# Three of eight weight pieces of each gate and up chunk as seven products of 256 columns, and norm weights applied ahead of the transposes

## The chip, the core and the metric

One core of one Trainium2 chip runs one launch of a two-layer decoder trunk. The metric is device time of the launch in microseconds (us), the median of several runs. The profile is one execution of the same program.

## What is computed

Two layers, 256 tokens of width 2048, float32. The mixers (attention and gated delta rule) are not touched here; what matters is the chain around them:

```python
def rms_norm(x, w):
    y = xf * lax.rsqrt(jnp.mean(xf * xf, axis=-1, keepdims=True) + NORM_EPS)
    return (y * w.astype(jnp.float32)).astype(x.dtype)

def swiglu(u, w_gate, w_up, w_down):
    return (jax.nn.silu(u @ w_gate) * (u @ w_up)) @ w_down

for layer in range(DEPTH):
    u = rms_norm(h, mix_norm_pre[layer])
    u = even_mixer(u, ...) if layer % 2 == 0 else odd_mixer(u, ...)
    h = h + rms_norm(u, mix_norm_post[layer])
    u = swiglu(rms_norm(h, ffn_norm_pre[layer]), ffn_w_gate[layer], ffn_w_up[layer], ffn_w_down[layer])
    h = h + rms_norm(u, ffn_norm_post[layer])
```

The gate and up matrices are 2048 x 5632, the down matrix 5632 x 2048.

## The kernel before

**Tiles.** The 256 tokens are two token tiles t = 0 and t = 1 of 128. A weight matrix is cut into chunks of 512 columns, and a chunk into pieces of 256 rows: a piece is 128 partitions x 2 x 512 float32, 512 KB, one DMA. A gate or up chunk has 8 pieces, and there are 11 of each per layer. `load_until` (L186) keeps up to WB = 10 pieces loaded ahead: SyncE (SP) loads a piece into one of RAW = 4 buffers `raw`, ScalarE copies it rounded into `wh` (L179), VectorE writes the rest `raw - wh` into `wl` (L180). Activations are split into a high and a low part in the same way.

**Products.** `step` (L198) takes one piece for one token tile: for each of its 2 blocks of 128 rows three matmuls of 512 columns, `xh wh` (L205), `xh wl` (L206) and `xl wh` (L207), all into the chunk's PSUM tile `acc`, of which there are 3. So a piece costs 12 matmuls of 512 columns for both token tiles. Each matmul loads its own weights, the 128 x 128 activation block.

**Order.** Six phases follow each other: mixer input, mixer output, feed-forward part (FFN), and the same for layer 1. `run_phase` (L228) lets t = 0 run 4 to 8 steps ahead of t = 1, so that what ends t = 0 can lie beside matmuls of t = 1. In the FFN, `plan_ffn` (L443) orders gate and up chunks in pairs and puts the four down chunks of the pair before behind the next gate chunk. The program is written in this order, and a scheduler of the language then orders each engine's instructions by priorities; each engine runs its own in that order.

**Between phases.** `post_residual` (L294) waits for the sums of squares of all four column tiles (`rms`, through GpSimd), adds the scaled result to x (L304), transposes x (L174) and splits it. The norm weight goes in there: after the transpose it is one number per partition, so `transposed` (L248) splits 16 pieces of 128 x 128 for a token tile, ScalarE at L182 and VectorE at L183. The factor 1/rms of the next norm (`prenorm_factor`, L261) isn't needed yet: it is applied to the outputs, in `gate_chunk` (L469) and `up_chunk` (L478) by `self.r[t]`. x stays in SBUF through the FFN.

**Chunk ends.** Gate: one SiLU on ScalarE (L469). Up: one multiply on VectorE (L478), four transposes (L174), a split. Down: one add on VectorE (L496).

## Time and profile before

| | us |
|---|---|
| median of 3 runs | 2458.36 (2457.79 to 2459.09) |
| the profiled execution | 2455.95 |
| its span in the trace | 2454.2 |
| TensorE busy in it | 2415.8 |
| VectorE busy in it | 1359.1 |
| ScalarE busy in it | 1137.3 |

The page gives busy time by engine, the span in 40 slices with the clock that TensorE was granted, and the chain of work that ended last. A matmul's row has its start and a modelled duration; the durations of neighbours overlap, so the cost of one is the distance from one start to the next. Windows are counted from the span's start: the first FFN runs from about 530 to 1286, the second from about 1688 to 2445.

### The profile page before, as it was taken

Reading aid. Unit: us, or ns where it says so; the run is one execution under the profiler, and the core shown is the slowest. Engines: PE = TensorE matmul, PEld = TensorE weight load, DVE = VectorE, ACT = ScalarE, POOL = GpSimd, SP = SyncE. Lnnn points to the kernel's source line nnn. Section 1 sums busy time; section 2 is a strip of 40 time slices with the busy share of each in tenths; the row PEclk is TensorE's granted clock in tenths of the full one; section 3 lists DMA queues with packets and bytes.
Section 4 is the critical chain, followed back from the end, with each engine's and each line's share of the span. In section 5 each row is a group of like instructions: output and inputs, shape, how many; then the busy total and the mean of one; then the engine's idle time right before and its main releaser. Section 6 shows DMA issues by size and latency. Waiting matters only on the chain.

```text
span 2454.2 us, 29318 instructions
## 1 busy us (share of the span) xinstructions
PE 2415.8 (98%) x11076; PEld 1969.2 (80%) x11076; DVE 1359.1 (55%) x1767; ACT 1137.3 (46%) x1558; POOL 189.5 (8%) x212
## 2 busy tenths in 40 slices
...
GB/s 238 209 136 149 142 138 151 146 176 197 183 186 189 181 189 187 185 185 188 193 209 194 163 176 172 200 198 144 204 185 184 184 184 194 180 189 185 186 195 129
DMA packets 128078, 441.90 MB, mean 180 GB/s; under 512 B 14848, under 2 KB 20224, under 8 KB 127936
## 3 DMA queue, kind: packets, MB, share of 16 engines
...
HBM read 435.77 MB, written 4.19 MB: 179 GB/s over the span
## 4 chain that ended last, share of the span: by engine, by line
PE 90%; POOL 2%; DVE 2%; issue 2%; DMA 2%; ACT 1%; POOLq 0%; ACTq 0%; DVEq 0%; SPq 0%
PE acc L207 28%; PE acc L205 28%; PE acc L206 28%; PE p L174 2%; POOL m L838 1%; POOL m L840 1%; PE p L932 1%; ACT wh L179 1%; DVE wl L180 0%; DVE m L304 0%; DMA raw<-in_ev_w_in 0%; PE p L660 0%; PE p L687 0%; PE p L941 0%; POOL m L501 0%
## 5 line engine op out<-in xcount | busy, mean ns | idle before, releaser
L180 DVE TENSOR_TENSOR wl<-raw,wh 128x1024 fp32r<-128x1024 f32 (+1 forms) x808 | 990.7, 1229 | 854.9 <-ACT wh L179 852.9
L179 ACT ACTIVATE wh<-raw 128x1024 fp32r<-128x1024 f32 (+1 forms) x808 | 848.6, 1051 | 956.9 <-PE acc L207 924.9
L205 PE MATMUL acc<-wh,m 128*128 128x512 f32 (+1 forms) x3232 | 1276.7, 396 | 10.7 <-ACT m L182 10.4
L207 PE MATMUL acc<-wh,m 128*128 128x512 f32 (+1 forms) x3232 | 1272.6, 396 | 4.1 <-DVE m L183 4.1
L206 PE MATMUL acc<-wl,m 128*128 128x512 f32 (+1 forms) x3232 | 1274.0, 395 | 0.0
L205 PEld LDWEIGHTS acc<-wh,m 128*128 128x128 f32 x3232 | 609.5, 189 | 151.1 <-ACT m L182 14.2
L207 PEld LDWEIGHTS acc<-wh,m 128*128 128x128 f32 x3232 | 609.5, 189 | 147.3 <-DVE m L183 8.5
L206 PEld LDWEIGHTS acc<-wl,m 128*128 128x128 f32 x3232 | 609.5, 189 | 138.1
L277 POOL DMA_DIRECT2D m<-in_ffn_norm_post x16 | 9.0, 562 | 1405.1 <-PE acc L207 1319.6
L496 DVE TENSOR_TENSOR m<-m,acc 128x512 f32<-128x512 f32 x80 | 54.8, 685 | 61.4 <-PE acc L207 61.4
L174 PE MATMUL p<-ident,m 128*128 128x128 f32 x528 | 77.4, 275 | 1.0 <-ACT m L874 0.6
L174 PEld LDWEIGHTS p<-ident,m 128*128 128x128 f32 x528 | 64.5, 142 | 14.3 <-ACT m L874 1.3
L179 ACT ACTIVATE m<-p 128x512 fp32r<-128x512 f32 x44 | 26.3, 598 | 72.9 <-PE p L174 72.7
L180 DVE TENSOR_TENSOR m<-p,m 128x512 fp32r<-128x512 f32 x44 | 30.4, 691 | 44.1 <-ACT m L179 44.1
L469 ACT ACTIVATE m<-acc,pr 128x512 f32<-128x512 f32 x44 | 30.4, 690 | 45.8 <-PE acc L207 45.8
L290 ACT ACTIVATE m<-m 128x512 f32<-128x512 f32 x48 | 30.1, 628 | 43.6 <-DVE m L496 37.4
L182 ACT ACTIVATE m<-p,nw 128x128 fp32r<-128x128 f32 x128 | 38.6, 376 | 14.3 <-PE p L174 8.7
L561 ACT ACTIVATE m<-acc,pr 128x512 f32<-128x512 f32 x36 | 24.8, 689 | 42.6 <-PE acc L207 42.5
L183 DVE SCALAR_TENSOR_TENSOR m<-p,nw,m 128x128 fp32r<-128x128 f32 x128 | 38.0, 343 | 6.7 <-ACT m L182 6.3
L478 DVE SCALAR_TENSOR_TENSOR m<-acc,pr,m 128x512 f32<-128x512 f32 x44 | 32.9, 748 | 9.6 <-PE acc L207 9.6
L846 DVE SCALAR_TENSOR_TENSOR m<-c,conv,m 128x128 f32<-128x128 f32 x96 | 30.6, 378 | 0.0
L932 PE MATMUL p<-m,m 128*128 128x128 f32 x112 | 20.7, 303 | 8.2 <-POOL m L917 7.7
...
## 6 DMA issues: line engine op xcount, KB each, us to landing
raw<-in_ffn_w_gate SPq DMA_DIRECT2D x176, 512.0 KB, 3.3
raw<-in_ffn_w_up SPq DMA_DIRECT2D x176, 512.0 KB, 3.3
raw<-in_ffn_w_down SPq DMA_DIRECT2D x176, 512.0 KB, 3.3
raw<-in_ev_w_in SPq DMA_DIRECT2D x104, 512.0 KB, 3.9
raw<-in_od_w_in SPq DMA_DIRECT2D x96, 512.0 KB, 3.3
raw<-in_ev_w_out SPq DMA_DIRECT2D x32, 512.0 KB, 4.3
raw<-in_od_w_out SPq DMA_DIRECT2D x32, 512.0 KB, 4.3
...
```

The costliest lines, as they stand in the source:

```text
L174: self.nc.tensor.transpose(o[:, j * P:(j + 1) * P], src[:, j, :], self.ident)
L179: self.nc.scalar.activation(h, src, AF.Copy)
L180: self.nc.vector.tensor_sub(l, src, h.bitcast(F32))
L182: self.nc.scalar.activation(h, src, AF.Copy, scale=scale)
L183: self.nc.vector.scalar_tensor_tensor(l, src, scale, h.bitcast(F32), op0=ALU.mult, op1=ALU.subtract)
L205: nc.tensor.matmul(acc, xh, s.wh[:, j], start=(s.first and j == 0), stop=False)
L206: nc.tensor.matmul(acc, xh, s.wl[:, j], start=False, stop=False)
L207: nc.tensor.matmul(acc, xl, s.wh[:, j], start=False, stop=(s.last and j == 1))
L478: nc.vector.scalar_tensor_tensor(u, acc, self.r[t], u, op0=ALU.mult, op1=ALU.mult)
L496: nc.vector.tensor_add(y, y, acc)
L846: nc.vector.scalar_tensor_tensor(dst[:, h], c[:, h, j:j + P], w[:, j:j + 1], dst[:, h] if j else self.zero, op0=ALU.mult, op1=ALU.add)
L932: mm(z[:, i * P:(i + 1) * P], M[:, i], self.blocks(Xt_, i, s, 1), start=True, stop=True)
```

## The change

Let a piece's two row blocks be split into column halves: B11, B12 for the first block, B21, B22 for the second, each 128 x 256, and let e and o be a token tile's two activation blocks. Strassen's algorithm in Winograd's form gets the products of both token tiles with all four from 7 products instead of 8. 3 of the 8 pieces (NSP) of all gate and up chunks but each layer's first gate chunk go this way (`FastChunk`, `fast_step`), 63 pieces per layer. `split_sums` makes the three weight sums in the `raw` tile with 512, 256 and 256 columns on VectorE; the split then goes over 1792 columns rather than 1024, and the piece takes two of the 10 weight places. The other operand's four sums are made once per layer for 3 pieces in `sums_of_tiles` and transposed (12 transposes of 128 x 128 per layer). A fast step is for both token tiles at once: 7 x 3 matmuls of 256 columns, into 4 PSUM tiles. At the end of a chunk the parts are put together by one copy on ScalarE and six adds on VectorE.

For the sums the activations must be normed whole before the transposes. So the norm weights come in as rows broadcast over partitions (`norm_weights`, through a DRAM tile `nwd` that the start fills), and `post_residual` multiplies by them ahead of the transposes; towards the FFN it multiplies by the factor 1/rms too, so that `prenorm_factor` now stands ahead of the transposes. The boundary splits are then 512 columns wide. `post_residual` gets a high priority (LEAD). `raw` tiles are twice as wide and 3 rather than 4; the SBUF tiles are 44 rather than 48; x is stored to DRAM at the end of a mixer output and loaded again late in the FFN. In an FFN phase three PSUM tiles are lent from the pool `ps` to the pool of accumulators, and given back after the phase.

```diff
-NTILES = 48
+NORMS = (("mix_norm_pre", 0), ("mix_norm_pre", 1), ("ffn_norm_pre", 0), ("ffn_norm_pre", 1))
+NTILES = 44
 NPS = 5
 PSA = 3
-RAW = 4
+RAW = 3
+NSP = 3
+LEAD = 500
+PS_FFN = 3
...
+class FastChunk(Chunk):
+    def __init__(self, pieces, lhs, done):
+        super().__init__(pieces[NSP:], lhs, done)
+        for s in self.steps:
+            s.last = False
+        self.steps += [Step(s, k, self, i == 0, i == NSP - 1, i) for i, (s, k) in enumerate(pieces[:NSP])]
...
+    def lend(self, other):
+        i = self.free.pop()
+        make = self.make if isinstance(i, int) else i[0]
+        other.free.append((make, i if isinstance(i, int) else i[1]))
...
-    def load_until(self, n):
-        nc = self.nc
-        while self.loaded < min(n, len(self.steps)):
+    def load_until(self, n, end=None):
+        nc = self.nc
+        while self.loaded < min(n + WB if end is None else end, len(self.steps)):
             s = self.steps[self.loaded]
-            n_ = s.src.shape[2]
-            raw, wh, wl = (p.tile([P, 2, 512], dt, name=tag, tag=tag)[:, :, :n_] for p, dt, tag in (
-                (self.rpool, F32, "raw"), (self.wpool, F32R, "wh"), (self.wpool, F32R, "wl")))
-            nc.sync.dma_start(out=raw, in_=s.src)
-            self.split(wh, wl, raw)
-            s.wh, s.wl = wh, wl
+            if sum(a.places for a in self.steps[n:self.loaded + 1]) > WB:
+                break
+            raw = self.rpool.tile([P, 2048], F32, name="raw", tag="raw")
+            w = [self.wpool.tile([P, 2048], F32R, name="w", tag="w") for i in range(s.places)]
+            if s.pair is None:
+                n_ = s.src.shape[2]
+                raw = raw[:, :1024].rearrange("p (k n) -> p k n", k=2)[:, :, :n_]
+                s.wh, s.wl = (a.rearrange("p (k n) -> p k n", k=2)[:, :, :n_] for a in (w[0][:, :1024], w[0][:, 1024:]))
+                nc.sync.dma_start(out=raw, in_=s.src)
+                self.split(s.wh, s.wl, raw)
+            else:
+                nc.sync.dma_start(out=raw[:, :1024], in_=s.src.rearrange("p k n -> p (k n)"))
+                self.split_sums(raw.rearrange("p (b n) -> p b n", b=8), s, *w)
             self.loaded += 1
+    def split_sums(self, b, s, wh, wl):
+        nc = self.nc
+        nc.vector.tensor_sub(b[:, 4:6], b[:, 0:1].broadcast_to([P, 2, 256]), b[:, 1:3])
+        nc.vector.tensor_sub(b[:, 6], b[:, 1], b[:, 5])
+        nc.vector.tensor_sub(b[:, 7], b[:, 3], b[:, 6])
+        s.wh, s.wl = (a.rearrange("p (b n) -> p b n", b=8)[:, :7] for a in (wh, wl))
+        self.split(s.wh, s.wl, b[:, 1:8])
     def step(self, t, s):
         nc, ch = self.nc, s.chunk
         if s.first:
...
+    def fast_step(self, s):
+        nc, ch = self.nc, s.chunk
+        if s.first:
+            ch.p16, ch.p57 = self.now(self.pa, 2)
+        lo, hi = slice(0, 256), slice(256, 512)
+        ke, ko = s.kts
+        B11, B22, B21, T1, T3, T2, T4 = range(7)
+        S = lambda i: tuple(a.bitcast(F32R)[:, s.pair * P:s.pair * P + P] for a in self.S[i])
+        products = ((ch.p16[:, lo], ch.lhs(0, ke), B11), (ch.p16[:, hi], S(1), T2),
+                    (ch.p57[:, lo], S(0), T1), (ch.p57[:, hi], S(2), T3),
+                    (ch.acc[0][:, hi], ch.lhs(0, ko), B21), (ch.acc[0][:, lo], S(3), B22),
+                    (ch.acc[1][:, hi], ch.lhs(1, ko), T4))
+        for i, (acc, (xh, xl), b) in enumerate(products):
+            kw = dict(skip_group_check=True)
+            nc.tensor.matmul(acc, xh, s.wh[:, b], start=s.first and i in (0, 2), stop=True, **kw)
+            nc.tensor.matmul(acc, xh, s.wl[:, b], start=False, stop=True, **kw)
+            nc.tensor.matmul(acc, xl, s.wh[:, b], start=False, stop=True, **kw)
+        if s.last:
+            za, zb, zu = self.now(self.mem, 3)
+            u = zu[:, lo]
+            nc.scalar.activation(za[:, hi], ch.p16[:, lo], AF.Copy)
+            nc.vector.tensor_add(u, za[:, hi], ch.p16[:, hi])
+            nc.vector.tensor_add(za[:, lo], u, ch.p57[:, lo])
+            nc.vector.tensor_add(zb[:, hi], u, ch.p57[:, hi])
+            nc.vector.tensor_add(zb[:, lo], zb[:, hi], ch.p57[:, lo])
+            self.mem.give(zu)
+            out = [za, zb]
+            for z, acc in zip(out, ch.acc):
+                nc.vector.tensor_add(z, z, acc)
+            self.pa.give(ch.p16, ch.p57, *ch.acc)
+            ch.done(out)
         self.advance()
...
+            if n0 < hi and self.steps[n0].pair is not None:
+                if n0 == n1:
+                    self.fast_step(self.steps[n0])
+                    n0 += 1
+                    n1 += 1
+                    self.load_until(n1)
+                    continue
+                lag = 0
...
+    def transposed(self, src, n=4):
+        o = self.now(self.ps)
+        for j in range(n):
+            self.nc.tensor.transpose(o[:, j * P:(j + 1) * P], src[:, j * P:(j + 1) * P], self.ident)
+        h, l = self.now(self.mem, 2)
+        self.split(h.bitcast(F32R)[:, :n * P], l.bitcast(F32R)[:, :n * P], o[:, :n * P])
+        self.ps.give(o)
+        return h, l
+    def sums_of_tiles(self, xn):
+        nc = self.nc
+        tiles = self.now(self.mem, 4)
+        S = [a[:, :NSP * P].rearrange("p (i d) -> p i d", d=P) for a in tiles]
+        for c in range((NSP + 1) // 2):
+            n = min(2, NSP - 2 * c)
+            (e0, o0), (e1, o1) = ([v4(xn[t][c]).rearrange("p (i k) d -> p i k d", k=2)[:, :n, j] for j in range(2)]
+                                  for t in range(2))
+            s1, s2, s3, s4 = (a[:, 2 * c:2 * c + n] for a in S)
+            nc.vector.tensor_add(s1, e1, o1)
+            nc.vector.tensor_sub(s2, s1, e0)
+            nc.vector.tensor_sub(s3, e1, e0)
+            nc.vector.tensor_sub(s4, o0, s2)
+        self.S = []
...
-    def post_residual(self, t, norm):
+    def norm_weights(self, which, layer):
+        self.nwb = self.now(self.mem, 4)
+        for c in range(4):
+            self.norm_weight(self.nwb[c], which, layer, c)
+    def post_residual(self, t, then):
         nc = self.nc
         self.free_aT(t)
@@ -302,14 +444,31 @@
         for c in range(4):
             x, y = self.x[t][c], self.y[t][c]
             nc.vector.scalar_tensor_tensor(x, y, rf, x, op0=ALU.mult, op1=ALU.add)
-            self.mem.give(y)
-            if norm is None:
+            if then == "out":
                 nc.sync.dma_start(out=self.out[t * P:(t + 1) * P, c * 512:(c + 1) * 512], in_=x)
-            else:
-                self.transposed(t, c, norm)
-        self.y[t] = None
-        if norm is not None:
+            elif then == "in":
+                nc.vector.tensor_mul(y, x, self.nwb[c])
+                self.aT[t].append(self.transposed(y))
+            if then != "ffn":
+                self.mem.give(y)
+        if then != "out":
             self.prenorm_factor(t)
+        if then == "ffn":
+            for c in range(4):
+                y = self.y[t][c]
+                nc.vector.scalar_tensor_tensor(y, self.x[t][c], self.r[t], self.nwb[c], op0=ALU.mult, op1=ALU.mult)
+                self.aT[t].append(self.transposed(y))
+            if t == 1:
+                self.sums_of_tiles(self.y)
+                for b in range(2):
+                    self.mem.give(*self.y[b])
+        if t == 1 and then != "out":
+            self.mem.give(*self.nwb)
...
-        for (lo, hi), end in zip(bounds, ends):
+        for i, ((lo, hi), end) in enumerate(zip(bounds, ends)):
+            if i % 3 == 2:
+                for j in range(PS_FFN):
+                    self.ps.lend(self.pa)
+                if i == 2:
+                    self.mem.give(*self.lev)
             self.run_phase(lo, hi, end)
+            if i % 3 == 2:
+                for j in range(PS_FFN):
+                    self.pa.lend(self.ps)
...
+    def fast(name, f):
+        return f > 0 or name == "ffn_w_up"
...
+        self.nc.scalar.activation(self.sg[t], acc, AF.Silu)
+    def gate_fast(self, out):
+        self.sg = out
+        for a in out:
+            self.nc.scalar.activation(a, a, AF.Silu)
     def up_chunk(self, t, i, acc):
-        nc = self.nc
-        if i == 0:
-            for pair in self.hT[t]:
-                self.mem.give(*pair)
-            self.hT[t] = []
         u = self.sg[t]
-        nc.vector.scalar_tensor_tensor(u, acc, self.r[t], u, op0=ALU.mult, op1=ALU.mult)
-        o = self.now(self.ps)
-        self.transpose4(o, v4(u))
+        self.nc.vector.tensor_mul(u, acc, u)
+        self.hT[t].append(self.transposed(u))
...
+    def up_fast(self, i, f, out):
+        if f == NFC - 1:
+            self.free_S()
+            for t in range(2):
+                self.free_aT(t)
+        for t in range(2):
+            self.up_chunk(t, i, out[t])
+            self.mem.give(out[t])
...
-        self.post_residual(t, None if layer else 1)
+        with self.tc.high_priority(offset=LEAD):
+            self.post_residual(t, "out" if layer else "in")
         if layer == 0:
-            for c in range(4):
-                self.nc.sync.dma_start(out=self.xd[t * P:(t + 1) * P, c * 512:(c + 1) * 512], in_=self.x[t][c])
-            self.mem.give(*self.x[t])
+            self.store_x(t)
...
-        self.post_residual(t, 2 + layer)
+        with self.tc.high_priority(offset=LEAD):
+            self.post_residual(t, "ffn")
+        self.store_x(t)
...
```

**TensorE, from the first FFN into the second layer's mixer.** p_10107 to p_10155 and p_10788 to p_10810 are transposes of t = 0; the rows ahead of them are t = 1's last matmuls of the down chunk, those behind them t = 0's first of the mixer. Before:

```order
L206 MATMUL acc<-wl,m_9871 128x512
L207 MATMUL acc<-wh,m_9872 128x512
L174 MATMUL p_10107<-ident,m_4192 128x128 x4
L174 MATMUL p_10123<-ident,m_4193 128x128 x4
L174 MATMUL p_10139<-ident,m_4194 128x128 x4
L174 MATMUL p_10155<-ident,m_4195 128x128 x4
L205 MATMUL acc<-wh,m_10112 128x512
L206 MATMUL acc<-wl,m_10112 128x512
L207 MATMUL acc<-wh,m_10113 128x512
```

With the change:

```order
L263 MATMUL p_10905<-w,m_10513 128x512
L364 MATMUL p_10788<-ident,m_10570 128x128 x4
L364 MATMUL p_10799<-ident,m_10660 128x128 x4
L261 MATMUL acc_11034<-w,m_10793 128x512
L262 MATMUL acc_11034<-w,m_10793 128x512
L261 MATMUL acc_11103<-w,m_10793 128x512
L262 MATMUL acc_11103<-w,m_10793 128x512
L364 MATMUL p_10810<-ident,m_10742 128x128 x4
L263 MATMUL acc_11034<-w,m_10794 128x512
```

Four transposed tiles stood in a row, each in a PSUM tile of its own; now two stand there, and the third, which takes the first one's PSUM tile, stands behind four matmuls and ahead of the first use of a low half.

**VectorE, from the first mixer output into the first FFN.** This is the end of t = 0: x is made (L304, L446), and the low halves of its transposes (L183 before, L218 with p in it now) are written. acc at L549 and acc_4643 at L752 are t = 1's last chunk. Before:

```order
L304 SCALAR_TENSOR_TENSOR m_4194<-m_4596,prf,m_4194 128x512
L304 SCALAR_TENSOR_TENSOR m_4195<-m_4703,prf,m_4195 128x512
L180 TENSOR_TENSOR wl<-raw,wh 128x1024 x3
L163 TENSOR_SCALAR pj,pv<-xss 128x5
L180 TENSOR_TENSOR wl<-raw,wh 128x1024
L183 SCALAR_TENSOR_TENSOR m_4725<-p_4719,nw,m_4724 128x128
```

With the change:

```order
L446 SCALAR_TENSOR_TENSOR m_4068<-m_4560,prf,m_4068 128x512
L218 TENSOR_TENSOR w<-raw,w 128x1024 x3
L201 TENSOR_SCALAR pj,pv<-xss 128x5
L190 SCALAR_TENSOR_TENSOR pna<-pny,pv 128x1
L194 TENSOR_SCALAR pna<-pna 128x1
L396 TENSOR_TENSOR pr<-pny,pna 128x1
L459 SCALAR_TENSOR_TENSOR m_4081<-m_4065,pr,m_4073 128x512
L459 SCALAR_TENSOR_TENSOR m_4297<-m_4066,pr,m_4074 128x512
L459 SCALAR_TENSOR_TENSOR m_4457<-m_4067,pr,m_4075 128x512
L459 SCALAR_TENSOR_TENSOR m_4560<-m_4068,pr,m_4076 128x512
```

```order
L218 TENSOR_TENSOR w<-raw,w 128x1024 x2
L201 TENSOR_SCALAR pj,pv<-xss 128x5
L752 TENSOR_TENSOR m_4727<-acc_4643,m_4727 128x512
L218 TENSOR_TENSOR m_4606<-p_4600,m_4605 128x512
```

The second fence follows the first without a gap: between x and the first low half there now stand the whole second norm, four multiplies and t = 1's last output tile.

**VectorE, in the middle of the first FFN.** m_6216 is an up chunk's output before; m_10289 and m_10290 are the two token tiles' outputs of a gate chunk now. Before:

```order
L496 TENSOR_TENSOR m_5647<-m_5647,acc 128x512
L180 TENSOR_TENSOR wl<-raw,wh 128x1024 x5
L478 SCALAR_TENSOR_TENSOR m_6216<-acc,pr,m_6216 128x512
L180 TENSOR_TENSOR wl<-raw,wh 128x1024 x2
L180 TENSOR_TENSOR m_6677<-p_6671,m_6676 128x512
```

With the change:

```order
L218 TENSOR_TENSOR w<-raw,w 128x1024 x3
L292 TENSOR_TENSOR m_10291<-m_10289,acc_10210 128x256
L247 TENSOR_TENSOR raw<-raw 128x512
L293 TENSOR_TENSOR m_10289<-m_10291,p_10211 128x256
L294 TENSOR_TENSOR m_10290<-m_10291,p_10211 128x256
L248 TENSOR_TENSOR raw<-raw 128x256
L247 TENSOR_TENSOR raw<-raw 128x512
L299 TENSOR_TENSOR m_10289<-m_10289,p_10119 128x512
L295 TENSOR_TENSOR m_10290<-m_10290,p_10211 128x256
L249 TENSOR_TENSOR raw<-raw 128x256
```

The next chunk's weight sums (L247 to L249) now stand among the adds that wait for the chunk's last matmuls.

## Rows read from the trace of the kernel before

**Rows 1.** The page: TensorE, its weight loads, VectorE, ScalarE and GpSimd over the span.

```profile
PE 2415.8 (98%) x11076; PEld 1969.2 (80%) x11076; DVE 1359.1 (55%) x1767; ACT 1137.3 (46%) x1558; POOL 189.5 (8%) x212
```

**Rows 2.** Window inside the first FFN: each engine's busy time, granted clock, DMA.

```profile
core 0: us, PE busy (x) PEld busy (x) DVE busy (x) ACT busy (x) POOL busy (x), PEclk, DMA share, GB/s
550.00:1280.00 730.00, 730.00 (x3181) 589.29 (x3180) 372.39 (x346) 307.64 (x323) 12.45 (x15) 1.00 0.57 187
```

**Rows 3.** Timeline of TensorE in the first FFN: start, duration, matmuls of 512 columns.

```profile
799.68 0.40 PE L205 MATMUL acc<-wh,m 128*128 128x512 f32 x1
...
805.99 0.39 PE L205 MATMUL acc<-wh,m 128*128 128x512 f32 x1
```

**Rows 4.** Timeline of TensorE in the first mixer: matmuls of 256 columns, two stretches.

```profile
77.48 0.28 PE L205 MATMUL acc<-wh,m 128*128 128x256 f32 x1
...
80.77 0.28 PE L206 MATMUL acc<-wl,m 128*128 128x256 f32 x1
...
81.59 0.28 PE L205 MATMUL acc<-wh,m 128*128 128x256 f32 x1
...
84.31 0.28 PE L205 MATMUL acc<-wh,m 128*128 128x256 f32 x1
```

**Rows 5.** Chain of waits: eight matmuls of 128 columns (start, time on the chain).

```profile
1378.38 0.89 PE p L687 x8
```

**Rows 6.** Groups by line and shape, VectorE and ScalarE: count, busy us, mean ns.

```profile
L180 DVE TENSOR_TENSOR wl<-raw,wh 128x1024 fp32r<-128x1024 f32 x792 | 979.6, 1239 | 853.8 <-ACT wh L179 851.7
L180 DVE TENSOR_TENSOR wl<-raw,wh 128x544 fp32r<-128x544 f32 x8 | 5.8, 720 | 0.3 <-ACT wh L179 0.3
L674 DVE TENSOR_TENSOR m<-m,sd 128x512 f32<-128x512 f32 x12 | 8.3, 692 | 0.4
L934 DVE TENSOR_TENSOR m<-p,m 128x256 f32<-128x256 f32 x28 | 11.8, 420 | 6.2 <-PE p L932 6.0
L179 ACT ACTIVATE wh<-raw 128x1024 fp32r<-128x1024 f32 x792 | 838.3, 1060 | 947.1 <-PE acc L207 915.5 <-DMA raw<-in_ev_w_in 11.3 <-DMA raw<-in_od_w_out 4.0
L179 ACT ACTIVATE wh<-raw 128x544 fp32r<-128x544 f32 x8 | 5.3, 658 | 5.3 <-PE acc L207 4.8 <-DMA raw<-in_ev_w_abz 0.5
```

**Rows 7.** DMA issues: KB each, median us from issue to landing.

```profile
raw<-in_ffn_w_gate SPq DMA_DIRECT2D x176, 512.0 KB, 3.3
raw<-in_od_w_out SPq DMA_DIRECT2D x32, 512.0 KB, 4.3
```

**Rows 8.** Windows at the three phase boundaries around an FFN.

```profile
529.00:541.00 12.00, 9.19 (x39) 6.49 (x38) 11.86 (x34) 9.91 (x27) 2.12 (x4) 0.86 0.78 263
1286.00:1299.00 13.00, 9.97 (x38) 6.75 (x37) 13.00 (x36) 10.60 (x30) 6.99 (x6) 0.74 0.86 307
1687.00:1700.00 13.00, 10.44 (x41) 7.31 (x40) 12.77 (x36) 10.81 (x30) 2.00 (x3) 0.78 0.70 240
```

**Rows 9.** TensorE's timeline at the first: sixth and nineteenth matmul behind the transposes.

```profile
532.40 0.39 PE L207 MATMUL acc<-wh,m 128*128 128x512 f32 x1
...
540.61 0.39 PE L205 MATMUL acc<-wh,m 128*128 128x512 f32 x1
```

**Rows 10.** Timeline of VectorE at the same place: start, time, instructions.

```profile
519.96 0.69 DVE L549 TENSOR_TENSOR m<-acc,m 128x512 f32<-128x512 f32 x1 [4.82 <-ACT m L290]
...
524.28 2.73 DVE L304 SCALAR_TENSOR_TENSOR m<-m,prf,m 128x512 f32<-128x512 f32 x4
526.93 3.49 DVE L180 TENSOR_TENSOR wl<-raw,wh 128x1024 fp32r<-128x1024 f32 x3
...
531.55 0.86 DVE L183 SCALAR_TENSOR_TENSOR m<-p,nw,m 128x128 fp32r<-128x128 f32 x3
```

**Rows 11.** Timeline at the start: SP's weight loads, VectorE's first weight split.

```profile
8.14 1.62 SPq L193 DMA_DIRECT2D raw<-in_ev_w_in  x2
...
9.24 1.22 DVE L180 TENSOR_TENSOR wl<-raw,wh 128x1024 fp32r<-128x1024 f32 x1 [9.24 <-ACT wh L179]
...
13.04 2.62 SPq L193 DMA_DIRECT2D raw<-in_ev_w_in  x2
```

100 lines of the change are left out of this document (70 added, 30 removed).

## The prediction

> **What bounds the kernel now.** I read the page's busy times first: TensorE is busy for 98% of the span, no other engine for more than 55% [rows 1]. Then a window inside the first FFN, where the change acts: TensorE is busy for all of its 730 us, at a granted clock of 1.00, which is the upper of its two levels, 2.4 GHz, while VectorE works 372 us of them, 51%, and the DMA engines 57% [rows 2]. So in the FFN the time is the number of matmuls times the distance between two. That distance comes from the timeline: from 799.68 to 805.99 there are 27 steps, so 0.2337 us for 512 columns [rows 3]; over longer stretches it comes out at 0.233, which I use. Last I looked where TensorE does wait near an FFN: at the three boundaries around it, where its share falls to 77 to 80% and its mean clock to 0.74 to 0.86 [rows 8]. There VectorE is the one that is busy, 98 to 100% of the window.
>
> **The products.** A piece now takes 12 matmuls of 512 columns: 12 x 0.233 = 2.80 us. A fast piece takes 21 of 256 columns. The trace has such matmuls, each with its own weight load and with the same pattern of operands (the same block twice, then its low part): 28 steps from 77.48 to 80.77 make 0.1175 us, 24 steps from 81.59 to 84.31 make 0.1133 [rows 4]. I take 0.1165, half of 0.233 and nearer to the slow stretch: 21 x 0.1165 = 2.45 us. That is 0.35 us less per piece, and for 2 layers x 21 chunks x 3 = 126 pieces 44 us; with the two measured ends it is 42 to 53 us. TensorE was without a gap there, so all of it lies on the path, if the operands are there in time.
>
> **A rule against it.** Matmuls of 128 columns, a quarter of 512, come every 0.111 us (0.89 us for eight) [rows 5], not every 0.058, so something other than columns has a floor there, and 256 columns lie just above it. The Trainium skill, "TensorE: Matmul & The Clock Gate", section "LDWEIGHTS (loading the stationary operand)", gives a load of 128 columns 128/1.2 = 107 ns. By that the load fills nearly the whole of a 256-column matmul, and were it not hidden the gain would turn into a loss (second rival below); if hidden, the sum stays at -44 us. The two stretches of rows 4 speak for hidden.
>
> **What TensorE gets in addition.** 12 transposes of the activation sums per layer and one of the norm weights: 25 x 0.111 [rows 5] = +2.8 us, on its path.
>
> **The boundaries.** The first costs 5.2 us: from 532.40 to 540.61 there are 13 steps, 8.2 us where 3.0 would do [rows 9]. For the others I add TensorE's idle time (3.0 and 2.6 us) and half of the time at the lower level, 1.2 GHz: a mean of 0.74 over 13 us is 6.8 us of it, 0.78 is 5.7 [rows 8]. That makes 6.4 and 5.5, and 17 for all three. What decides is when VectorE writes the first low halves, since L207, now L263, waits for them. t = 0's last output is taken up at 519.96 and x is written from 524.28 on, behind a norm with two weight splits in it; then come three splits (3.49 us) and one more, and the first low quarter at 531.55 [rows 10]. In the new order those two splits are gone from the norm, so x starts 2.3 us earlier, at 522.0. Then follow four x (2.73), three splits (3.49), the second norm with its trip through GpSimd (3.6 us from 520.65 to 524.28 for the first, less its two splits: 1.3), four multiplies (2.7), two splits (2.3), t = 1's output (0.7) and the low half (0.7): 535.9, some 4 us later than before. But it is a whole 512 columns then, and the next three follow 0.7 to 1.8 us apart, where the 16 small pieces kept TensorE waiting again and again. So TensorE waits in one piece of about 4 us, and gets the lower clock behind it as before: I put this at +1.5 us at each of the two mixer-output boundaries. Behind the FFN the third transpose needs the first one's PSUM tile, which is free only after that tile's split; the queue up to there holds six weight splits (7.0 us), eight tiles of x and y (5.4), three adds and two multiplies of outputs (3.4), a norm (1.3) and the split (0.7): some 18 us after t = 0's last matmul, of which t = 1's 39 matmuls cover 9. That is some 7 us idle beside the transposes, and up to 3.4 lost at the lower clock, against 6.4 before: +4. Together +7. The bounds are -9 (the priority clears VectorE's queue and half of the 17 us go) and +16 (twice my delay).
>
> **The start.** The fourth weight load now waits until the first buffer is free, at about 10.5 rather than 8.1, and what stands behind it on SP, two x tiles and the fifth load (13.04 before), moves by as much [rows 11]. TensorE waits for x there: +2 us, between 0 and 4. In the mixers the loads have 3 buffers too, but the order of their small matmuls among the large is within a few steps of before: 0, within 3 either way.
>
> **Weights in time.** This is what a fast chunk hides behind matmuls, and it costs nothing only while VectorE keeps up. A chunk takes TensorE 60 x 0.233 + 63 x 0.1165 = 21.3 us. VectorE: a fast piece needs 0.69 + 0.42 + 0.42 for the sums, and a split of 1792 columns, by 1239 and 720 ns at 1024 and 544 columns about 2.05: 3.6 us; three of them and five ordinary splits (1.24) make 17.0 us; the chunk's end four adds of 256 and two of 512 columns, 3.1; an up chunk two multiplies and two splits more, 2.8 [rows 6]. That is 20 to 23 us in durations, some 8% less in sequence, since three splits in a row take 3.49 us, not 3.72 [rows 10]. So VectorE is full while four fast chunks follow each other, and has its pause in the four down chunks behind them (45 us of matmuls, about 25 of VectorE). What lies ready ahead is ten places, some six pieces or 15 us. A raw tile is held for 3.3 (landing [rows 7]) + 1.5 + 1.7 (ScalarE's 1060 and 658 ns carried on to 1792) + 2.05 = 8.6 us by a fast piece, 5.6 by another [rows 6]: 54 us per chunk over 3 tiles, 18 against 21.3. It fits by a little; I give it +2 us, between 0 and 12. The reloads of x and norm weights go through GpSimd's queue, which has 190 us of work in the whole span [rows 1], a group ahead of their use: 0. The stores of x stand on SP ahead of weight loads, but wait only for x, which is early: 0.
>
> **Sum.** -44 + 2.8 + 7 + 2 + 2 = -30. The profiled execution took 2455.95 us (its span 2454.2 and 1.75 around it), the median is 2.4 above it: 2458.4 - 30 = 2428 us.
>
> **Rivals.** First, the boundaries get cheaper: rows 8 show VectorE at 98 to 100% there, with weight splits among it, and the boundary's own work has become 12 wide operations from 20 small and wide ones per token tile. At -9 instead of +7 the time is 2412 us. Against it: the order still has five splits ahead of the first low half. Second, the load isn't hidden behind 256 columns: then a product takes 0.1165 + 0.111 = 0.228 us, a piece 4.8, and the time is 2428 + 126 x 2.3 = about 2720 us; from 2.80/21 = 0.133 per product on the change does not do what it says and nothing is gained. Rows 4 speak against both. Third, and slower: VectorE and the three raw tiles become the bound in the fast chunks. A piece that waits one and a half times for another's split holds its tile for 3.1 us more, which makes 26 us per chunk; four in a row are late by 19 us, of which the lead hides some 10, eleven such runs give +100: about 2530 us. It is slower than before from some 24.5 us per chunk on. For it: VectorE at 92 to 100% by my sum, and a landing of 4.3 us is seen elsewhere [rows 7]. Against it: splits of the next chunk stand ahead of TensorE's need by some 6 us in the order, and DMA is busy 57% [rows 2]. A mild form of it, 5 to 25 us, gives 2435 to 2453.
>
> **How the numbers follow.** Forecast 0.64; cheaper boundaries 0.17; the mild form of the third rival 0.10, its strong form 0.07; loads not hidden 0.02. The forecast's own bounds, with products at -53 to -42, boundaries from 0 to +16, start, mixers and weights at their ends, reach from 2415 to 2446. The range takes in the first rival and leaves out the strong third, the second and the upper part of the mild one: 2410 to 2447. Faster by over 0.2% (4.9 us, about what a measurement of this kernel can tell from no change) is the forecast, the first rival and nearly all of the mild form: 0.88; within 0.2% 0.04; slower 0.08.
>
> **What would show it.** Steps of 0.113 to 0.118 us at L285 to L287 at a clock of 1.00, and TensorE without gaps in the FFN windows, VectorE there at about 80%: right. A row of TensorE waiting for VectorE at L287 or L285 behind a chunk's third piece: the third rival. At the boundaries one wait of 3 to 5 us for L218, 7 behind the FFN, with a clock of 0.7 to 0.9 behind it: right; none: the first rival. Most likely wrong is the boundaries' sum, since it hangs on when weight splits are ready; what would break the forecast is a fast chunk above 21.3 us.

## The result and the profile after

The changed kernel takes 2477.59 us (median of 4 runs, 2473.97 to 2480.75) against 2458.69 for the kernel before: a ratio of 1.0077, 95% interval 1.0059 to 1.0094. It is 19 us slower; 30 us faster was forecast, and the range ended at 2447. The profiled execution took 2476.57 us (span 2474.8), 20.6 more than that of before.

From the page after, the lines that answer to [rows 1] and [rows 7], and the shares of the chain of work that ended last:

```profile
PE 2393.2 (97%) x12235; PEld 1992.8 (81%) x12235; DVE 1725.7 (70%) x2373; ACT 1205.3 (49%) x1537; POOL 201.3 (8%) x241
PE 28%; DMA 24%; DVE 19%; ACT 6%; issue 4%; ACTq 0%; POOL 0%; DVEq 0%; POOLq 0%
DVE w L218 12%; DMA raw<-in_ffn_w_gate 9%; DMA raw<-in_ffn_w_down 8%; DMA raw<-in_ffn_w_up 7%; ACT w L217 6%; PE acc L263 5%; PE acc L261 5%; PE acc L262 5%; PE p L263 3%; PE p L262 3%; PE p L261 3%; DVE m L299 1%; DVE raw L247 1%; DVE raw L248 1%; DVE raw L249 1%
raw<-in_ffn_w_gate SPq DMA_DIRECT2D x176, 512.0 KB, 4.2
```

The chain's shares by engine before:

```profile
PE 90%; POOL 2%; DVE 2%; issue 2%; DMA 2%; ACT 1%; POOLq 0%; ACTq 0%; DVEq 0%; SPq 0%
```

TensorE is still busy for 97% and no other engine for more than 70%, so the first line hides what happened. The chain shows it: 90% of its time was TensorE's before, now 28% is; weight loads have 24% and weight splits 18% (12 on VectorE, 6 on ScalarE). A load lands after 4.2 us where it took 3.3.

The fast products are there and as cheap as forecast. TensorE's timeline inside a fast chunk, the first and the last of 63 rows (start, modelled duration):

```profile
791.00 0.28 PE L285 MATMUL acc<-w,m 128*128 128x256 f32 x1
...
798.04 0.28 PE L287 MATMUL acc<-w,m 128*128 128x256 f32 x1
```

62 steps in 7.04 us are 0.1135 each; the mean over the run is 0.115. What the page can't show is where TensorE waited. I took, for every matmul of the trace, the step to the next one's start less what it takes undisturbed (0.233 us for 512 columns, 0.115 for 256, 0.123 for 272, 0.111 for 128), and added it up by stretch of the span. A wait and the lower clock behind it are both in it. With three of the kernels that follow:

| lost by TensorE, us | before | b_raw3_nt44 | a_nofast | after | a_raw4 |
|---|---|---|---|---|---|
| start (0 to 60) | 9.4 | 8.0 | 8.6 | 8.6 | 8.6 |
| mixer and its output (60 to 500) | 25.5 | 40.6 | 39.6 | 41.2 | 29.6 |
| first boundary (500 to 560) | 5.0 | 7.3 | 4.5 | 4.4 | 7.1 |
| inside the first FFN (560 to 1230) | -0.2 | 0.0 | -0.5 | 13.9 | -1.6 |
| its last down chunks, FFN to mixer (1230 to 1400) | 6.4 | 18.1 | 7.0 | 22.0 | 8.6 |
| odd mixer, third boundary (1400 to 1740) | 6.1 | 6.3 | 5.8 | 4.4 | 5.8 |
| second FFN (from 1740) | -0.6 | -0.4 | 0.4 | 22.2 | 0.2 |
| sum | 51.6 | 80.0 | 65.4 | 116.7 | 58.2 |

TensorE lost 65 us more than before and had 45 less to do. Its waits in after, by what ended them: us in total, times, longest.

```profile
PE p L364 <- DVE m L450: 7.0, 1, 7.0
PE p L261 <- ACT w L217: 5.7, 1, 5.7
PE acc L261 <- ACT w L217: 5.6, 2, 4.8
PE p L364 <- DVE m L666: 5.5, 4, 2.4
PE acc L364 <- DVE m L666: 4.0, 4, 1.7
```

Two of these are weights that came late in the last down chunks of each FFN (L261 for L217, 4.8 and 5.7 us). The eight of L364 for L666 recur once in each pair of gate and up chunks, some 135 us apart: the product of gate and up is late on VectorE. In a_raw4 below, the first kind has 0.3 us left and the second nothing.

**One late load.** SP, VectorE and ScalarE around the end of that fast chunk; the loads and subtractions are those of the next chunk's fast pieces (timeline; in brackets the idle time ahead and what ended it):

```profile
794.46 4.59 SPq L240 DMA_DIRECT2D raw<-in_ffn_w_gate  x3
807.06 10.94 SPq L237 DMA_DIRECT2D raw<-in_ffn_w_up  x5
...
801.31 0.69 DVE L247 TENSOR_TENSOR raw<-raw 128x512 f32<-128x512 f32 x1 [0.69 <-DMA raw<-in_ffn_w_gate]
801.92 0.41 DVE L293 TENSOR_TENSOR m<-m,p 128x256 f32<-128x256 f32 x1
802.25 0.41 DVE L294 TENSOR_TENSOR m<-m,p 128x256 f32<-128x256 f32 x1
802.58 0.42 DVE L248 TENSOR_TENSOR raw<-raw 128x256 f32<-128x256 f32 x1
803.14 0.69 DVE L247 TENSOR_TENSOR raw<-raw 128x512 f32<-128x512 f32 x1
803.75 0.68 DVE L299 TENSOR_TENSOR m<-m,acc 128x512 f32<-128x512 f32 x1
804.34 0.41 DVE L295 TENSOR_TENSOR m<-m,p 128x256 f32<-128x256 f32 x1
804.67 0.42 DVE L249 TENSOR_TENSOR raw<-raw 128x256 f32<-128x256 f32 x1
805.01 2.02 DVE L218 TENSOR_TENSOR w<-raw,w 128x1792 fp32r<-128x1792 f32 x1
...
805.18 1.70 ACT L217 ACTIVATE w<-raw 128x1792 fp32r<-128x1792 f32 x1 [2.76 <-DVE raw L249]
```

The piece whose first subtraction starts at 801.31 has its third one end at 805.09, 3.8 us later, though the three take 1.53: between them stand the adds of the chunk's end (L293 to L299) and the next piece's first subtraction. The three raw tiles are taken from 798.7 on, and SP issues no load until a split ends at 807.03: the next goes out at 807.06. From 60 us on nearly every load goes out 0.03 us after the split that frees its tile, so a tile's holding time is the distance from its issue to the third issue behind it. Over 560 to 1230 that is 13.24 us for the 63 fast pieces and 6.81 for the 172 others; the prediction had 8.6 and 5.6. A fast chunk's loads then take (3 x 13.24 + 5 x 6.81) / 3 = 24.6 us, TensorE 21.2. The four down chunks behind four fast ones win most of that back: their 16 loads hold a tile for 6.75 us each, 36.0 us over three tiles, for 44.7 us of TensorE. So a group of eight chunks falls 4 x 3.4 - 8.7 = 4.9 us short, and the five groups of an FFN some 25 us, an estimate from these means; against a_nofast the table has 29 us for the first FFN with the stretch behind it and 22 for the second.

### The profile page after: what moved, and what is told of

The parts are those of the page before. It is cut to its first block, busy times and chain, and to the rows that moved or that the text cites. A ratio compares the mean times of both kernels' runs of the same rounds, so it can differ in the third digit from the quotient of the medians.

```text
span 2474.8 us, 32450 instructions
## 1 busy us (share of the span) xinstructions
PE 2393.2 (97%) x12235; PEld 1992.8 (81%) x12235; DVE 1725.7 (70%) x2373; ACT 1205.3 (49%) x1537; POOL 201.3 (8%) x241
## 4 chain that ended last, share of the span: by engine, by line
PE 28%; DMA 24%; DVE 19%; ACT 6%; issue 4%; ACTq 0%; POOL 0%; DVEq 0%; POOLq 0%
DVE w L218 12%; DMA raw<-in_ffn_w_gate 9%; DMA raw<-in_ffn_w_down 8%; DMA raw<-in_ffn_w_up 7%; ACT w L217 6%; PE acc L263 5%; PE acc L261 5%; PE acc L262 5%; PE p L263 3%; PE p L262 3%; PE p L261 3%; DVE m L299 1%; DVE raw L247 1%; DVE raw L248 1%; DVE raw L249 1%
## 5 line engine op out<-in xcount | busy, mean ns | idle before, releaser
L218 DVE TENSOR_TENSOR w<-raw,w 128x1024 fp32r<-128x1024 f32 (+2 forms) x808 | 1085.7, 1350 | 551.8 <-ACT w L217 548.9
L217 ACT ACTIVATE w<-raw 128x1024 fp32r<-128x1024 f32 (+2 forms) x808 | 928.7, 1153 | 993.3 <-DVE raw L249 231.5
L261 PE MATMUL acc<-w,m 128*128 128x512 f32 (+2 forms) x1622 | 643.2, 397 | 14.6 <-ACT w L217 5.6
L262 PE MATMUL acc<-w,m 128*128 128x512 f32 (+2 forms) x1622 | 640.4, 396 | 4.0 <-DVE w L218 3.9
L263 PE MATMUL acc<-w,m 128*128 128x512 f32 (+2 forms) x1622 | 639.9, 396 | 2.0 <-DVE m L218 1.2
L261 PE MATMUL p<-w,m 128*128 128x512 f32 x1106 | 439.8, 399 | 6.8 <-ACT w L217 5.7
L262 PE MATMUL p<-w,m 128*128 128x512 f32 x1106 | 439.3, 397 | 4.0 <-DVE w L218 3.7
L263 PE MATMUL p<-w,m 128*128 128x512 f32 x1106 | 438.5, 397 | 0.2 <-DVE m L218 0.2
L261 PEld LDWEIGHTS acc<-w,m 128*128 128x128 f32 x1622 | 307.6, 190 | 84.2 <-ACT w L217 7.9
L262 PEld LDWEIGHTS acc<-w,m 128*128 128x128 f32 x1622 | 307.5, 190 | 75.2 <-DVE w L218 9.4
L263 PEld LDWEIGHTS acc<-w,m 128*128 128x128 f32 x1622 | 307.5, 190 | 70.6 <-DVE m L218 1.8
L261 PEld LDWEIGHTS p<-w,m 128*128 128x128 f32 x1106 | 208.5, 189 | 56.4 <-ACT w L217 8.2
L262 PEld LDWEIGHTS p<-w,m 128*128 128x128 f32 x1106 | 208.7, 189 | 55.2 <-DVE w L218 8.2
L263 PEld LDWEIGHTS p<-w,m 128*128 128x128 f32 x1106 | 208.5, 188 | 49.6 <-DVE m L218 0.6
L286 PE MATMUL p<-w,m 128*128 128x256 f32 x480 | 133.3, 278 | 0.4 <-DVE w L218 0.4
L285 PE MATMUL p<-w,m 128*128 128x256 f32 x480 | 133.4, 278 | 0.0
L287 PE MATMUL p<-w,m 128*128 128x256 f32 x480 | 133.1, 277 | 0.0
L247 DVE TENSOR_TENSOR raw<-raw 128x512 f32<-128x512 f32 x126 | 86.9, 690 | 49.9 <-DMA raw<-in_ffn_w_up 32.2
L285 PE MATMUL acc<-w,m 128*128 128x256 f32 x402 | 111.9, 278 | 0.0
L286 PE MATMUL acc<-w,m 128*128 128x256 f32 x402 | 111.3, 277 | 0.0
L287 PE MATMUL acc<-w,m 128*128 128x256 f32 x402 | 111.3, 277 | 0.0
L286 PEld LDWEIGHTS p<-w,m 128*128 128x128 f32 x480 | 90.4, 188 | 1.6 <-DVE w L218 1.0
```

The lines of the kernel that those rows point to most:

```text
L217: self.nc.scalar.activation(h, src, AF.Copy)
L218: self.nc.vector.tensor_sub(l, src, h.bitcast(F32))
L247: nc.vector.tensor_sub(b[:, 4:6], b[:, 0:1].broadcast_to([P, 2, 256]), b[:, 1:3])
L261: nc.tensor.matmul(acc, xh, s.wh[:, j], start=(s.first and j == 0), stop=False)
L262: nc.tensor.matmul(acc, xh, s.wl[:, j], start=False, stop=False)
L263: nc.tensor.matmul(acc, xl, s.wh[:, j], start=False, stop=end)
```

## Experiments

Names with b_ are the kernel before with an edit, those with a_ the changed kernel with one. Ratios are to the kernel before on the same chip (2456.0 to 2458.1 us there). The theory: raw tiles are held too long for three of them, and this takes back the gain. Its rival: VectorE's work and order make weights late, and the tiles only show it. The runs were made on several chips, and the kernel before itself differs by 2 us among them, so a difference between medians of two chips is uncertain by about as much.

**b_raw3: three raw tiles alone.**

```diff
-RAW = 4
+RAW = 3
```

> The kernel before with three raw weight tiles instead of four, nothing else. After lost 13 us in the two mixers and at the first boundary, where none of its fast products run. Theory A (three raw tiles make weights late wherever a load is slow): this alone brings some 10 us, 2466 to 2472 us, most of it in the mixers (trace 100 to 550 us), and its FFN windows stay without stalls, since an ordinary piece holds a tile for 5.6 us only. Theory B (VectorE's work and order make weights late, tiles are not the cause): within 2 us of before, 2457 to 2461.

Measured: 2467.22 us, ratio 1.0037 (1.0024 to 1.0050), +9.1. Theory: hit. TensorE lost 12.5 us more in the profiled execution than before, 6.7 of them in the mixer and its output, the rest at the start and the boundaries, none inside the FFNs.

**a_nofast: the change without the fast products.**

```diff
-        return f > 0 or name == "ffn_w_up"
+        return False
-                self.sums_of_tiles(self.y)
+                self.S = []
```

(and the activations are freed behind each token tile's last up chunk.)

> The changed kernel without fast chunks and without the sums of the activations: all eight pieces of each chunk in 12 matmuls, and norm weights ahead of the transposes, the new boundaries, three raw tiles of 8 KB and 44 tiles as in the changed kernel. TensorE's work is that of before. Theory A: mixers and boundaries keep their loss (13 and some 11), stalls in the FFNs go since VectorE has time: 2470 to 2485 us. Theory B: boundaries cost as forecast (+7), mixers nothing: 2462 to 2468. If the boundary edit is a gain in itself: below 2458.

Measured: 2470.54 us, ratio 1.0051 (1.0036 to 1.0066). The edits around the products cost 12.4 us by themselves, nearly all in the mixer (table above); waits inside the FFNs are gone. From here to the changed kernel it is +7.1 us, with 45.2 less of TensorE's work: the fast products bring 52 us of new waits.

**a_raw4: four raw tiles, the sums in tiles of their own, in the same space.**

```diff
-RAW = 3
+RAW = 4
+SUMS = 2
-raw = self.rpool.tile([P, 2048], F32, name="raw", tag="raw")
+raw = self.rpool.tile([P, 1024], F32, name="raw", tag="raw")
...
+c = self.spool.tile([P, 1024], F32, name="sums", tag="sums").rearrange("p (b n) -> p b n", b=4)
-self.split(s.wh, s.wl, b[:, 1:8])
+self.split(s.wh[:, :3], s.wl[:, :3], b[:, 1:4])
+self.split(s.wh[:, 3:], s.wl[:, 3:], c)
```

> The changed kernel with four raw tiles of 4 KB and a pool of two more tiles of 4 KB for the sums of the fast pieces (the same space in all); the split of a fast piece becomes two instructions on each engine, of 768 and 1024 columns. Theory A: the stalls in the FFNs (24 us), at the last down groups (14) and part of the mixers' loss (13) go: 2477.6 - 24 - 14 - 8 = 2432, between 2425 and 2445. Theory B: VectorE has 126 x 0.1 = 13 us more to do and the order is the same: 2475 to 2485.

Measured: 2414.52 us, ratio 0.9822 (0.9805 to 0.9838): 63 us faster than the changed kernel and 43.6 faster than before, below what I expected. Window inside its first FFN (columns as in [rows 2]):

```profile
560.00:1230.00 670.00, 670.00 (x3599) 570.14 (x3598) 528.76 (x697) 339.20 (x383) 9.58 (x18) 1.00 0.59 196
```

The same of the changed kernel:

```profile
560.00:1230.00 670.00, 659.81 (x3512) 554.56 (x3511) 512.23 (x628) 318.94 (x313) 0.60 (x2) 1.00 0.59 185
```

What ScalarE's splits waited for most in that window, in a_raw4:

```profile
ACT w L219 <- PE p L268: 84.7, 50, 5.7
```

And in the changed kernel:

```profile
ACT w L217 <- DVE raw L249: 118.2, 34, 8.8
```

TensorE is busy for all of the 670 us while VectorE does more than in the changed kernel (528.76 us for 512.23), so its load was not the bound. A split now waits for TensorE to give a place back, as in the kernel before: weights are ahead again. In the changed kernel only 12.6 us of ScalarE's waits for a split in this window are for TensorE.

**a_nosub: without the subtractions.**

```diff
-        nc.vector.tensor_sub(b[:, 4:6], b[:, 0:1].broadcast_to([P, 2, 256]), b[:, 1:3])
-        nc.vector.tensor_sub(b[:, 6], b[:, 1], b[:, 5])
-        nc.vector.tensor_sub(b[:, 7], b[:, 3], b[:, 6])
-        self.split(s.wh, s.wl, b[:, 1:8])
+        self.split(s.wh, s.wl, b[:, 1:2].broadcast_to([P, 7, 256]))
```

> The changed kernel without the three subtractions of each fast piece (its seven blocks are split all from one block, so the products are of wrong blocks): VectorE has 126 x 1.53 = 193 us less to do, and a fast piece holds its raw tile for 7.1 us instead of 8.6; three tiles remain. Theory A: the FFN's stalls shrink by about half and the last down group's stay: 2460 to 2470 us. Theory B: the FFN's stalls and those of the last down group go: 2477.6 - 24 - 12 = 2442, between 2436 and 2450.

Measured: 2432.06 us, ratio 0.9898 (0.9883 to 0.9913). My figure for the theory (2460 to 2470) was too high: I had counted only the subtractions' own 1.5 us, but what goes with them is the 4.1 us that they take among other work (mean from first subtraction to ScalarE's split in the changed kernel, 63 pieces). The time is below both brackets, and by itself this run speaks for the rival as much.

**a_raw3s2 and a_split2: which part of a_raw4 did it.** The first is a_raw4 with RAW = 3. The second is the changed kernel with nothing but the split in two instructions:

```diff
-        self.split(s.wh, s.wl, b[:, 1:8])
+        self.split(s.wh[:, :3], s.wl[:, :3], b[:, 1:4])
+        self.split(s.wh[:, 3:], s.wl[:, 3:], b[:, 4:8])
```

> a_raw4 with three raw tiles of 4 KB instead of four; the two tiles for sums and the split in two instructions stay. It parts the two things that a_raw4 did at once. In the trace of after a fast piece held its raw tile for 13.2 us and an ordinary one for 6.8, which makes (3 x 13.2 + 5 x 6.8) / 3 = 24.5 us per fast chunk against 21.3 of TensorE. Theory A (the number of raw tiles): a fast piece's raw tile comes free a little earlier, some 11 us, so the chunk needs some 22 us, and the mixers' +9 stays: 2448 to 2468 us. Rival (that the sums have their own space, and raw tiles come free before the split of the sums, is what helped): below 2430.

> The changed kernel with the split of a fast piece in two instructions on each engine (768 and 1024 columns), as in a_raw3s2, but raw tile and sums in one tile of 8 KB, of which there are three as in the changed kernel. It differs from a_raw3s2 only in that the raw tile is held until the split of the sums is done too. If the time a tile is held is the cause: 13 us or more per fast piece as in the changed kernel, 2470 to 2492 us. Rival (that two shorter instructions let ScalarE begin before the subtractions, and this is what gave 41 us): 2436 to 2448.

Measured: a_raw3s2 2436.70 us (0.9917, 0.9903 to 0.9932), a_split2 2465.87 (1.0036, 1.0023 to 1.0048). a_raw3s2 lies between its two brackets, a_split2 between its own two, so each thing had a part: of the 63 us, 22 are the fourth tile's. The rest parts into 29 for tiles that come free before the sums are split (a fast piece now holds one for 10.6 us, an ordinary one 7.4, which makes 23.0 per chunk, waits for places included) and 12 for the split in two. In a_split2 the holding time is that of the changed kernel (13.17), yet the time is 4 us below what I expected; of these 12 us half are in the FFNs, the rest in the mixers. Why there, I can't say.

Beside a_raw3s2, a_nosub does tell against VectorE's load. Its fast pieces hold a tile for 10.2 us, nearly as long, while VectorE has far less to do; the window inside the first FFN, a_raw3s2 first:

```profile
560.00:1230.00 670.00, 669.15 (x3603) 569.80 (x3602) 529.51 (x700) 340.54 (x386) 5.97 (x12) 1.00 0.60 192
560.00:1230.00 670.00, 669.97 (x3602) 570.10 (x3601) 447.47 (x448) 334.33 (x322) 8.60 (x16) 1.00 0.60 194
```

82 us less of VectorE's work in these 670 us, and by the measure of the table the two kernels lose nearly the same in the FFNs with the stretch behind the first: 21.7 and 20.5 us, where the changed kernel loses 58.1. The loss goes with the holding time; VectorE's load is at most a small part of it. (The two also differ in the split, which a_nosub does in one instruction.)

**b_raw3_nt44 and b_nt44: the boundary edit and the four tiles fewer.** In both `NTILES` is 44 for 48, in the first `RAW` is 3 too.

> The kernel before with three raw tiles and 44 tiles of 2 KB, the resources of a_nofast, from which it differs only by the norm weights ahead of the transposes, the moved stores and loads of x and the priority at the boundaries. a_nofast took 2470.5. If that edit costs what I forecast (+7): 2461 to 2466. If it costs nothing, and 44 tiles take what b_raw3 lacks to a_nofast (3 us): 2468 to 2472. If the edit is a gain: above 2473.

> The kernel before with 44 instead of 48 tiles of 2 KB and its four raw tiles. b_raw3_nt44 took 17.6 us more than b_raw3, most of it at the end of the even mixer (10.9 us of waits from 450 to 500 us) and behind the first FFN (9.8 more). If four tiles fewer cost this by themselves: 2470 to 2478 us. If only beside three raw tiles, since late tiles then hold up weight loads that have no slack: 2457 to 2464.

Measured: b_raw3_nt44 2484.82 us (1.0115, 1.0100 to 1.0130), b_nt44 2474.90 (1.0076, 1.0061 to 1.0091). Four tiles fewer cost 17.6 us beside three raw tiles and 18.9 alone, a cost that I had not seen at all. And the edit is a gain: a_nofast has the same resources as b_raw3_nt44 and is 14.3 us faster. Windows of b_nt44 at the end of the mixer and behind the first FFN:

```profile
440.00:500.00 60.00, 54.57 (x248) 43.70 (x247) 33.35 (x44) 30.62 (x44) 10.26 (x11) 0.94 0.49 156
1280.00:1320.00 40.00, 30.12 (x122) 22.62 (x121) 25.09 (x58) 21.25 (x49) 9.00 (x15) 0.83 0.61 205
```

The same of the kernel before:

```profile
440.00:500.00 60.00, 60.00 (x283) 49.37 (x283) 36.21 (x47) 34.32 (x53) 9.53 (x11) 1.00 0.54 171
1280.00:1320.00 40.00, 36.98 (x164) 28.88 (x163) 30.71 (x71) 26.72 (x64) 8.08 (x8) 0.91 0.58 197
```

With 44 tiles TensorE loses 5.4 and 6.9 us in these two windows, while VectorE and ScalarE are less busy than before, not more: no engine is overloaded there. Small matmuls of the mixer stand at other places of TensorE's order: of the 804 in the first 520 us that aren't weight matmuls, 408 stand behind another number of weight matmuls than before, the most moved 101 later (with three raw tiles alone 38, at most 20 away). That work which finds no tile is put off, and that this makes the waits, is argued, not shown.

**b_raw5: would the kernel before gain from a fifth raw tile?** (`RAW = 5`, `NTILES = 46`.)

> The kernel before with five raw tiles and 46 instead of 48 tiles of 2 KB. It tells whether a further raw tile is a gain of its own that has nothing to do with the fast products, so that a_raw4 stands beside a fair base. Theory A: in before TensorE waits for weights only at the start, so 2453 to 2459 us. If raw tiles are short there too: below 2450.

Measured: 2451.91 us, 0.9979 (0.9969 to 0.9988), between the two brackets: -5.7, of which I had expected next to none. It isn't a plain price of a fifth raw tile: with 46 tiles TensorE's order changes too (424 of the 804 moved, up to 80 earlier), and of the 4.8 us that it loses less in the mixer, 2.8 are a shorter wait for GpSimd. a_raw4 has four raw tiles, as before has, so none of its gain is shown to be of this kind.

**a_nofast_raw4: the products alone, with weights in time.** a_nofast with four raw tiles of 4 KB.

> a_nofast with four raw tiles (of 4 KB) instead of three of 8 KB. Against a_raw4 (2414.5) it differs by the fast products alone, against before by the boundary edit and 44 tiles. TensorE's work is 45 us more than a_raw4's; if the products' gain is now whole: 2456 to 2462 us. If a_raw4 still loses some of it to late weights: below 2455. If edit and fewer tiles together still cost against before: above 2463.

Measured: 2463.10 us, 1.0030 (1.0017 to 1.0042), on the edge of two brackets. a_raw4 is 48.6 us below it by the medians and 44.0 by the profiled executions, for 45.2 less of TensorE's work: the gain of the fast products, with their two tiles for sums and their transposes. Against b_nt44 it is 11.8 faster, the edit's gain with four raw tiles.

**a_raw4_lead0: without the priority at the boundaries.** (`LEAD = 0` for 500.)

> a_raw4 without the priority for the work at the ends of mixers and FFNs (LEAD 0 for 500). If the priority is what kept the boundaries at the cost of before although their chain has become longer, the three boundaries lose 2 to 5 us each: 2420 to 2430 us. If the chain itself, and not weight splits ahead of it, sets the wait: 2412 to 2418.

Measured: 2423.10 us, 0.9861 (0.9846 to 0.9876), 8.6 slower than a_raw4 by the medians, 4.8 between the profiled executions. Without the priority TensorE loses 3.2 us more at the first boundary and 3.9 in the stretch of the third, nothing more behind the FFN, and 3.6 less in the mixer and its output.

**Further: a_raw4_nsp4, a_raw4_pool, a_raw4_nsp4_pool, a_raw5s1.** Four fast pieces of eight (`NSP = 4`); two of the three subtractions on GpSimd; both; and five raw tiles with one for sums.

```diff
-        nc.vector.tensor_sub(c[:, 2], b[:, 1], c[:, 1])
-        nc.vector.tensor_sub(c[:, 3], b[:, 3], c[:, 2])
+        nc.gpsimd.tensor_sub(c[:, 2], b[:, 1], c[:, 1])
+        nc.gpsimd.tensor_sub(c[:, 3], b[:, 3], c[:, 2])
```

> a_raw4 with four fast pieces of eight. TensorE: 42 pieces more by 0.38 us = 16 us less, a chunk takes 48 x 0.233 + 84 x 0.115 = 20.8 us. VectorE: four fast pieces of 3.6 and four ordinary of 1.24 make 19.4, with the ends 22 to 25 us, more than 20.8 in runs of four chunks, with its pause in the down chunks behind. Theory A (tiles were the bound, VectorE still has room through its pauses): 2398 to 2406 us. Theory B (VectorE is the next bound): stalls of 2 to 4 us per chunk, 2420 to 2480.

> a_raw4 with the second and third subtraction of each fast piece on GpSimd instead of VectorE: VectorE has 126 x 0.84 = 106 us less to do, and the chain of the three becomes longer (GpSimd took 1.3 to 2 us for 512 columns in the mixers, so some 0.8 us for 256 against 0.42). Theory A (with four tiles neither VectorE nor the hold is the bound): within 4 us of a_raw4, 2410 to 2418. If VectorE is still short in the fast chunks: 2400 to 2409. If the longer chain brings the tile bound back: above 2420.

> a_raw4_nsp4 with the same two subtractions on GpSimd: VectorE 168 x 0.84 = 141 us less. a_raw4_nsp4 took 2409.5, 11 us less TensorE work than its gain shows, of which its FFNs lost 4 to 5 us to stalls. If VectorE is what is short there: 2402 to 2407. If not: within 3 us of 2409.5.

> a_raw4 with five raw tiles and one tile for sums, in the same space. The kernel before gained 5.7 us by a fifth raw tile. If raw tiles are still what is short outside the FFNs, and one sums tile is enough: 2406 to 2411 us. If fast pieces now wait for each other's sums (a tile of sums is held from the first subtraction to the end of its split, some 5 us by three pieces in a row, 2.45 us of TensorE each): 2420 to 2440.

Measured: 2409.54 us (0.9799, 0.9783 to 0.9815), 2419.99 (0.9846, 0.9831 to 0.9860), 2460.72 (1.0013, 1.0004 to 1.0022) and 2417.54 (0.9843, 0.9828 to 0.9857). None lies inside a bracket: the first, second and fourth lie between two, the third above both. Four fast pieces give 5 us of the 15 that TensorE saves: by the measure of the table it loses 7.4 us more than a_raw4, 4.5 of them inside the FFNs and 2.0 at the start. The kernel with four fast pieces is still the fastest of this study, 2% below before. GpSimd's help is a loss: 5 us with three fast pieces, 51 with four. A fifth raw tile at the price of a sums tile gives nothing.

## Why the prediction was wrong

Step by step, as it put them:

- **Products, -44: right, a little too small.** TensorE's work fell by 45.2 us with the transposes in it (+2.8), so the products alone take 48 less. In time, with the transposes, a_raw4 is 44.0 to 48.6 us below a_nofast_raw4, where 41.2 was forecast for both terms. The second rival is out: the step is 0.115 us. The formula of the Trainium skill ("TensorE: Matmul & The Clock Gate", section "LDWEIGHTS (loading the stationary operand)") makes 107 ns of a load of 128 columns, an estimate. It agrees with 128-column matmuls that come every 0.111 us, each with a load, and behind 256 columns the load is hidden.
- **Weights in time, +2 (0 to 12): this is the step that failed.** It is 52 us (a_nofast to after: +7.1 for -45.2 of work). The mis-sized terms are those of the holding time: landing 4.6 us to the first subtraction for 3.3, and 4.1 us from there to ScalarE's split for 1.5, since I added durations as though the three subtractions ran back to back, while each stood in VectorE's queue behind other work; 0.8 more goes ahead of VectorE's part of the split. 13.2 instead of 8.6 turns 18 us per chunk into 24.6. The prediction named the point, "some 24.5 us per chunk", at which the third rival decides, and gave its mild form 5 to 25 us: the mechanism was the right one, its place too, its chance too low and its price half of what it was. The rival's other half, that VectorE's load is the bound, is not: see a_nosub and a_raw4. Its sign, TensorE waiting at L285 or L287, hardly shows; the late weights are waited for at L261 and L262, in ordinary pieces, and at L364.
- **The reloads through GpSimd's queue, 0: wrong in this company.** The DMA issues between 1245 and 1258 us of the changed kernel (KB each, median us to landing):

```profile
raw<-in_ffn_w_down SPq DMA_DIRECT2D x4, 512.0 KB, 7.4
m<-xd POOLq DMA_DIRECT2D x6, 256.0 KB, 8.9
m<-nwd POOLq DMA_DIRECT2D x4, 256.0 KB, 9.5
m<-in_ffn_norm_post POOLq DMA_DIRECT2D x2, 256.0 KB, 8.2
```

The window of the wait there:

```profile
1250.00:1258.00 8.00, 3.19 (x13) 2.21 (x11) 3.86 (x4) 3.45 (x4) 2.69 (x5) 0.92 1.02 397
```

  Twelve transfers of x and norm weights fill the DMA engines (share 1.02), and weight loads land after 7.4 us instead of 4.2, at a place where no weights lie ready: TensorE waits 4.8 us here and 5.7 in the second FFN. a_raw4 issues the same burst and loses 0.5 us, with loads that take up to 11.0 us, since its weights lie ready. Its window:

```profile
1225.00:1233.00 8.00, 7.69 (x34) 5.90 (x33) 4.51 (x8) 1.27 (x3) 2.69 (x5) 1.00 1.02 378
```

  So the reloads cost next to nothing by themselves; they cost where weights have no lead.
- **Boundaries, +7: wrong; beside the kernel before it is 0.** The three stretches with a boundary lose 4.5, 7.0 and 5.8 us in a_nofast and lost 5.0, 6.4 and 6.1 before. The first rival (cheaper boundaries, -9) didn't come true either. That the edit is worth -14.3 us with the same tiles is for the most part the stretch behind the first FFN: the kernel before loses 18.1 us there with 44 tiles, a_nofast 7.0. The priority isn't what does it: it is worth 5 to 9 us in a_raw4, at the two other boundaries. Which of the edit's other parts it is, no run shows. The wait of "some 7 us" behind the first FFN stands in the trace of the changed kernel to the tenth (7.0, L364 for L450), but not for the reason given: a_nofast has the same work there and waits 0.7 us for L450. A late weight load is in it, on ScalarE:

```profile
1294.35 0.68 DVE L695 TENSOR_TENSOR m<-m,acc 128x512 f32<-128x512 f32 x1
...
1297.48 1.06 ACT L217 ACTIVATE w<-raw 128x1024 fp32r<-128x1024 f32 x1 [4.30 <-DMA raw<-in_od_w_in]
1298.45 0.62 ACT L426 ACTIVATE m<-m 128x512 f32<-128x512 f32 x1
```

  t = 0's last output is ready at 1295.03, but its squares (L426), which the norm waits for, stand behind a weight split whose load is late, and start 3.4 us later; in a_nofast they start 0.03 us behind the output. I had the number by chance.
- **Mixers, 0 within 3, and the start, +2: wrong.** The mixer and its output lost 15.7 us more, the start 0.8 less (with three raw tiles alone it lost 1.7 more, about as forecast). Three raw tiles cost 9.1 us in all and 44 tiles 17.6. The second has no term in the prediction: the diff's line on it was read as a change of space. And the order of the small matmuls is not "within a few steps of before": of the 804 in the first 520 us, 464 moved, the farthest by 125 weight matmuls, in a_nofast as in the changed kernel.
- **The arithmetic.** The bounds of the terms, added with each at its end, reach from 2405 to 2454 us and not from 2415 to 2446, and three splits in a row are 6% shorter than their durations, not 8% (3.49 for 3.72 us). Neither changes the outcome: the measured time is beyond either range.

In order of edits: 2458.1, +9.1 (three raw tiles), +17.6 (44 tiles), -14.3 (boundary edit), +7.1 (products: -45.2 of work, +52 of waits) = 2477.6.

What isn't settled: why the split in two saves 12 us with an unchanged holding time, by what path four tiles fewer cost 18 us and the boundary edit saves most of it, and why a load takes 4.2 us to land in the kernels with fast pieces and four or three raw tiles and 3.3 in those without; the loads go out in bunches there, but no run changed that alone.
